# A normalising row carried to all partitions through memory: one matrix product, a store and a load in place of eight spreading products, in a conv and RG-LRU mixer layer

## The chip, the cores and the metric

The kernel runs on one core of a Trainium2 chip. Its time is the device time of the core in microseconds, the median of several executions. The engines are named as in the profile: PE is TensorE (its weight loads stand apart as PEld), DVE is VectorE, ACT is ScalarE, POOL is GpSimd and SP is SyncE. Each engine takes its instructions in order from a queue of its own, and so does each DMA queue (SyncE's, ScalarE's and GpSimd's).

## The reference

One layer, a sequence of 1024 tokens, 1024 channels, everything in float32. `c` is one vector, so `shift`, `scale` and `gate` are one number per channel, the same for all tokens.

```python
mod = silu(c) @ mod_w + mod_b
shift, scale, gate = split(mod, 3)
h = x * rsqrt(mean(x*x, axis=-1) + EPS) * norm_g * (1 + scale) + shift
cv, cg, cs, lx, ls = split(h @ w_in, 5)             # 1024 columns each
v = silu(layernorm(causal_depthwise_conv(cv * sigmoid(cg), 31 taps)))
y_conv = (v @ pw2_w + pw2_b) * silu(cs)
xs = causal_depthwise_conv(lx, 4 taps)              # RG-LRU: gates r, i from block-diagonal
y_lru = linear_scan(a(r), b(i, xs)) * silu(ls)      # products of xs, then a scan over tokens
x = x + (1 + gate) * (concat(y_conv, y_lru) @ w_out)
return rmsnorm(x, final_g)
```

What matters for this case is the first normalisation. It has one factor per token, 1/std = rsqrt(mean(x*x) + EPS), which depends on the whole row of x, and two numbers per channel, `gs` = norm_g * (1 + scale) and `shift`.

## The kernel before, in words

**Layout.** Channels lie on the 128 partitions and tokens along the free axis. x is eight tiles `x0` to `x7` of 128x1024, loaded transposed. A column tile of `h @ w_in` (128 output channels, called a slot: `cg0` is the first tile of the conv GLU gate, `cv0` of the conv value, and so on) is a sum over the eight channel tiles, in two halves of 512 tokens; each half fills one PSUM bank of 128x512. TensorE does an fp32 product as three products of a shorter type: an operand is cut into a high part and the rest (`whi`, `wlo` for weights, `uh`, `ul` for the input), and high by high, high by low and low by high are summed. A half of a slot is thus 8 x 3 = 24 products of 128x512. ScalarE makes `whi` (L336), VectorE or GpSimd the difference `wlo` (L363).

**Normalising after the product.** The first seven slots do not wait for 1/std. The tiles `uh_k` and `ul_k` hold gs * x, not normalised, made as soon as an x tile and its `gs` are there. The product of a slot with them is then multiplied, when it leaves its bank, by `rbc`: a tile of 128x1024 in which every partition holds the row of 1/std of all 1024 tokens. The part of `shift` is the same number for all tokens of an output channel; it comes from a sum of its own (`fsum` on VectorE and ScalarE, a product with ones into the bank `psbias`, copied to `bias`) and is added as a bias where the slot is used.

- The first four slots (`FIRST`: cg0, cv0, cg1, cv1, numbered 0 to 3) are computed while x and the weights are still being loaded (L774, `fw_mm`), each x tile going into all of them as it arrives. Slots 0 to 2 have two banks each, `first0_0`, `first0_1` and so on; slot 3 has one, `first3`, for its first half. With the bank of the token statistics, `token_stats`, all eight banks are taken. The second half of slot 3 is the bank `late` (24 products of L774), which follows when another bank is free. In the code this is "`(a, e) in cuts[i]`": true for the halves with a bank of their own; `len(cuts[i]) == 1` is slot 3.
- Their banks are emptied by VectorE (L363): `first_u<-first,rbc`, one multiply for each 128x512, and one for `late`.
- Three further slots (`NEXT`, `next4` to `next6`, banks `ps4_0` and so on, L494) go the same way, `next<-ps,rbc`.
- From the seventh slot on the input is the normalised one: VectorE writes x := x * gs * rbc (L355, `x<-x,gs,rbc`), ScalarE `uh` := x + shift (L344) and VectorE `ul` := x + shift - uh (L355), into the same sixteen tiles.

**1/std.** The squares of x are summed over the tiles; products with a column of ones (L910) give, for each of eight blocks of 128 tokens, one column of `token_stats`: token p of block b at partition p, column b. ScalarE takes the root, VectorE the reciprocal `st` (128x8). Then `spread_mm` (L916) brings it to all partitions:

```python
pe.matmul(psb()[:, o:o + P], st[:, b:b + 1].to_broadcast([P, P]), ident, start=True, stop=True)
```

The stationary operand is one column of `st` repeated 128 times, the moving operand the identity, so the result has the block's 128 values along the free axis, the same on every partition. Four of these fill the bank; ScalarE copies 128x512 to `rbc` (`rbc<-token_stats`), and the other four follow in the same bank.

**Order of the work.** The kernel is a list of operations, each with its engine, an estimated duration, what it reads and writes, and a priority (a number; `RSP` = -110, `HHP` = -40, `EVP` = -80 and the due times of the loads are such numbers). A list scheduler runs over them when the program is built: each time an engine is free in its model, it takes the ready operation with the lowest number. What comes out is a fixed order for every queue, and the assignment of the eight banks and of the 47 buffers of 128x1024 to the tiles in turn. On the chip only the order and the waits are left. So an operation whose number or duration is changed may change places with others, on other engines too. `lag` adds a delay to the estimate of an operation's result, `slack` lets an operation be put into a queue ahead of the time at which the model has its inputs ready.

**Weights and SyncE.** Weight tiles (`raw`, 512 KB), the tiles `modw` for `shift` and `gate` (512 KB, one dot product on VectorE each, L355 `modw<-modw,sc`), and small gate tiles (`graw`) come in on SyncE's queue in the order in which the scheduler puts them there.

Of the kernel before, what the change touches and what calls it, by code (L numbers as in the profile page):

```python
# [9 lines left out]
F32 = mybir.dt.float32  # L10
F32R = mybir.dt.float32r
AF = mybir.ActivationFunctionType
ALU = mybir.AluOpType

P = 128
D = 1024
T = 1024
KT = D // P
# [18 lines left out]
START = ((0, H), (H, T))  # L37
# [44 lines left out]
TAPP = 15  # L82
TP = -60
SCALE = ("DVE", "DVE", "DVE", "DVE", "DVE", "DVE", "DVE", "DVE")
SQP, RSP, BIP, HHP, HCH, EVP = -84, -110, -50, -40, 0.1, -80


LOADS = "s0 a0 w0 s1 b0 w1 x1 W2 s2 x2 s3 x3 W4 s4 x4 s5 x5 W6 s6 x6 s7 x7 h0 h1 h2 h3 h4 h5 h6 h7".split()
# [205 lines left out]
def hymba_layer(ctx: ExitStack, tc: tile.TileContext, xT, vecs, mod_w, w_first, w_in,  # L294
# [3 lines left out]
    act, dve, pool, pe, sp = nc.scalar, nc.vector, nc.gpsimd, nc.tensor, nc.sync  # L298
# [7 lines left out]
    dram = ctx.enter_context(tc.tile_pool(name="dram", bufs=1, space=bass.MemoryType.DRAM))  # L306
# [11 lines left out]
    S = Plan(pools)  # L318
# [11 lines left out]
    def ACT(prio, out, in_, func, n=T, bias=None, scale=None, accum=None, r=(), w=(),  # L330
            reserve=0, after=()):
        kw = {}

        def emit():
            if func == "copy":
                act.copy(out(), in_())  # L336
                return
            if bias is not None:
                kw["bias"] = bias
            if scale is not None:  # L340
                kw["scale"] = scale
            if accum is not None:
                kw["accum_out"] = accum
            act.activation(out=out(), in_=in_(), func=func, **kw)  # L344
        ptr = sum(x is not None and not isinstance(x, float) for x in (bias, scale))
        return S.op("ACT", a_cost(n, ptr) + (0.1 if accum is not None else 0), emit, prio, r, w,
                    table=SETS.get(func), reserve=reserve, after=after)
# [12 lines left out]
    def TT(prio, eng, out, a, b, op, n=T, r=(), w=(), reserve=0, after=()):  # L360
        e = dve if eng == "DVE" else pool
        return S.op(eng, d_cost(n) if eng == "DVE" else p_cost(n),
                    lambda: e.tensor_tensor(out=out(), in0=a(), in1=b(), op=op), prio, r, w,  # L363
                    reserve=reserve, lock=not in_psum(r), after=after)
# [16 lines left out]
    def DMA(prio, out, in_, nbytes, r=(), w=(), after=(), reserve=0):  # L381
        return S.op("SP", max(0.1, nbytes / 360e3),
                    lambda: sp.dma_start(out(), in_()), prio, r, w, after=after,
                    reserve=reserve)
# [17 lines left out]
    def part(b, a, e):  # L402
        if isinstance(b, Two):
            z = a // H
            return part(b.b[z], a - z * H, e - z * H)
        return lambda: b()[:, a:e]

    def halves(b, a, e):
        if isinstance(b, Two):
            return [(b.b[z], 0) for z in (0, 1) if z * H < e and a < z * H + H]  # L410
        return [(b, i) for i in range(b.parts) if i * (T // b.parts) < e
                and a < (i + 1) * (T // b.parts)]

    FULL_BYTES = P * T * 4
# [9 lines left out]
    ident = const.tile([P, P], F32, tag="ident", name="ident")  # L424
# [305 lines left out]
    psb = bank("token_stats")  # L730
    cuts = [START, START, START, START[:1]]
# [55 lines left out]
    for i, ld in enumerate(LOADS):  # L787
        p = due[ld] = i - 100.0
# [5 lines left out]
        elif ld[0] in "wW":  # L794
            nk = 1 + (ld[0] == "W")
            rw, hi, lo = fw[k - k % 2]
            n, o, js = nk * FW, (k % 2) * FW, range(k % 2, k % 2 + nk)
            keys = lambda b: [(b, j) for j in js]
            DMA(p, part(rw, o, o + n), lambda k=k, n=nk: w_first[:, k:k + n, :], n * P * 4,
                w=keys(rw))  # L800
            for j in range(k, k + nk):
# [4 lines left out]
                if j:  # L806
                    SUB(p, "DVE", fw_part(lo, j), fw_part(rw, j), fw_part(hi, j), FW,
                        r=[(rw, jj), (hi, jj)], w=[(lo, jj)])
# [35 lines left out]
    for k in range(KT):  # L844
        p = due[f"s{k}"]
# [8 lines left out]
        p = max(p, due[f"x{k}"] if k else p, due[f"w{k}"])  # L854
# [4 lines left out]
        for a, e in START if k < UK else ((0, T),):  # L859
            n = e - a  # L860
            hk = halves(x_, a, e)
            if k == 0 == a:
                o = TS(p, part(uh, a, e), part(x_, a, e), g, None, ALU.mult, n=n,
                       r=hk + [("gs", k)], w=halves(uh, a, e))
            else:
                o = ACT(p, part(uh, a, e), part(x_, a, e), AF.Copy, n, scale=g,
                        r=hk + [("gs", k)], w=halves(uh, a, e))
            if k == 0 == a:
                rw, hi, lo = fw[0]
                SUB(p, "DVE", fw_part(lo, 0), fw_part(rw, 0), fw_part(hi, 0), FW,  # L870
                    r=[(rw, 0), (hi, 0), *halves(uh, a, e)], w=[(lo, 0)])
# [3 lines left out]
                r=hk + halves(uh, a, e) + [("gs", k)], w=halves(ul, a, e)))  # L875
# [3 lines left out]
        for z in range(3 if k == 0 else 0):  # L879
            for i, ps in enumerate(psf):  # L880
                o = fw_mm(p, ps, i, uh, ul, k, START[:1], z=z)
# [3 lines left out]
        for ch, (a, e) in enumerate(START):  # L885
            for i, ps in enumerate(psf):
# [3 lines left out]
                for z in range(3) if k < ZK else (None,):  # L890
                    o = fw_mm(q + 0.003 * (z or 0), ps, i, uh, ul, k, ((a, e),),
                              after=[begun[i, a // H]] if k == 0 and a % H else [], z=z)
# [3 lines left out]
    for k in range(KT):  # L896
        p = SQP + k
# [7 lines left out]
    rbc = big_buf("rbc", parts=4)  # L905
    st, wk = ctile("st", KT), [psb]
# [3 lines left out]
            pe.matmul(psb()[:, b:b + 1], sq()[:, b * P:b * P + P], ones[:, 0:1],  # L910
                      start=k == 0 and b == 0, stop=k == len(sqs) - 1, skip_group_check=True)

    def spread_mm(a, e):
        for b in range(a // P, e // P):
            o = b * P - a
            pe.matmul(psb()[:, o:o + P], st[:, b:b + 1].to_broadcast([P, P]), ident, start=True,  # L916
                      stop=True)
    for k, sq in enumerate(sqs):
        S.op("PE", 0.23 * KT, lambda sq=sq, k=k: stats(sq, k), RSP, [sq], wk, columns=4 * P * KT,
             after=[last_u[LASTK - 1, 3, 0]] if k else [])  # L920
    root = ACT(RSP, lambda: st, lambda: psb()[:, :KT], AF.Sqrt, KT, bias=eps_t,
               scale=1.0 / D, r=wk, w=[("st", 0)])
    S.op("DVE", 0.2, lambda: dve.reciprocal(st, st), RSP, [("st", 0)], [("st", 0)])
    for a, e in START:
        spread = S.op("PE", 0.22 * ((e - a) // P), lambda a=a, e=e: spread_mm(a, e), RSP,
                      [("st", 0)], wk, columns=4 * (e - a))
        spread_out = ACT(RSP, part(rbc, a, e), part(psb, 0, e - a), "copy", e - a, r=wk,
                         w=halves(rbc, a, e))


    fsum, bias = big_buf("fsum", parts=2), ctile("bias", len(FIRST + NEXT))
# [3 lines left out]
    for k in range(KT):  # L935
        p = due[f"h{k}"]
# [6 lines left out]
        if k == 0:  # L943
            ACT(p, facc, fw_part(rw, k), AF.Copy, FW, scale=shift[:, k:k + 1],
                r=[(rw, 0), ("shift", k)], w=[(fsum, 0)])
# [3 lines left out]
        for i, s in enumerate(NEXT):  # L949
            to, rw = part(fsum, FW + i * P, FW + i * P + P), raw[s]  # L950
            src = lambda rw=rw, k=k: k3(rw)()[:, k, :]
            if k == 0:
                ACT(p + 5, to, src, AF.Copy, P, scale=shift[:, k:k + 1],
                    r=[(rw, k), ("shift", k)], w=[(fsum, 1)])
# [5 lines left out]
    def shift_mm():  # L960
# [5 lines left out]
        w=[("bias", 0)])  # L966
# [311 lines left out]
    for i, (s, ps) in enumerate(zip(FIRST, psf)):  # L1278
        j, p, bi = s[1] % KT, EVP + i, bias[:, i:i + 1]
        t = big_buf(f"first_u{i}", parts=4)  # L1280
        for a, e in START:
            tk, pk, n = halves(t, a, e), halves(ps, a, e), e - a
            if (a, e) in cuts[i]:
                TT(p - 4 * (len(cuts[i]) == 1), "DVE", part(t, a, e), part(ps, a, e),
                   part(rbc, a, e), ALU.mult, n, r=pk + halves(rbc, a, e), w=tk)
            else:
                late = bank("late")
                for k in range(KT):
                    fw_mm(RSP + 60 + 0.1 * k, late, i, uhs[k], uls[k], k, ((a, e),),
                          after=[spread], off=a)  # L1290
                TT(p, "DVE", part(t, a, e), part(late, 0, n), part(rbc, a, e), ALU.mult, n,
                   r=[late] + halves(rbc, a, e), w=tk)
            if s[1] < CG:
                if a == 0:
                    v[j] = big_buf(f"v{j}")
                STT(p + 3, apart(v[j], a, e), by_two(t, a, e), bi, by_two(sig[j], a, e), ALU.add,
                    ALU.mult, n, r=tk + halves(sig[j], a, e) + [("bias", 0)], w=[v[j]])
        if s[1] >= CG:
            ACT(p + 3, t, t, AF.Sigmoid, bias=bi, r=[t, ("bias", 0)], w=[t])
            sig[j] = t  # L1300
# [6 lines left out]
    for s in slots[4:]:  # L1307
# [10 lines left out]
        ps = Two(f"ps{n}")  # L1318
# [243 lines left out]
```

## Time and profile before

| what | value |
|---|---|
| median of 3 runs | 733.07 us (733.06 to 733.56) |
| the profiled execution | 733.2 us, of which 731.4 us is the span in the trace |
| mean granted TensorE clock | 0.997 |
| ACT busy, instructions | 461.3 us (63%), 620 |
| TensorE: products of L494 on the chain that ends last | 65% of the span |
| HBM traffic | 64.16 MB read, 12.58 MB written |

How to read the views: the page begins with the busy time of each engine, its share of the span and its number of instructions. The list of waits has, for an engine, the operation that waited, what it waited for, the total time, how often, and the longest. The chain is the work that ended last, followed back from the last instruction: the start in us, the length, the engine, what it wrote and the line. A timeline row has the start, the busy time of the row, the engine, line, operation and tiles, the shape and the number of instructions, and in brackets the idle time before it and what ended that. A matmul's duration in a timeline includes its passage through the pipeline (0.39 us), so successive ones overlap, and the distance from start to start is what one costs. A DMA row has the queue, the count, the size of one and the median time in us from issue to landing. A row of windows has the window, its length, the busy time and instruction count of PE, PEld, DVE, ACT and POOL, the granted TensorE clock, the busy share of the DMA engines and their rate in GB/s.

### The profile page before, as it was taken

Reading aid. Unit: us, or ns where it says so; the run is one execution under the profiler, and the core shown is the slowest. Engines: PE = TensorE matmul, PEld = TensorE weight load, DVE = VectorE, ACT = ScalarE, POOL = GpSimd, SP = SyncE. Lnnn points to the kernel's source line nnn. Section 1 sums busy time; section 2 is a strip of 40 time slices with the busy share of each in tenths; the row PEclk is TensorE's granted clock in tenths of the full one; section 3 lists DMA queues with packets and bytes.
Section 4 is the critical chain, followed back from the end, with each engine's and each line's share of the span. In section 5 each row is a group of like instructions: output and inputs, shape, how many; then the busy total and the mean of one; then the engine's idle time right before and its main releaser. Section 6 shows DMA issues by size and latency. Waiting matters only on the chain.

```text
span 731.4 us, 8952 instructions
## 1 busy us (share of the span) xinstructions
PE 722.9 (99%) x3284; PEld 601.5 (82%) x3284; DVE 640.4 (88%) x912; ACT 461.3 (63%) x620; POOL 98.0 (13%) x107
## 2 busy tenths in 40 slices
PE   9999999999999999999999999999999999999996
PEld 8888888888888888888888888888888888887885
DVE  6999999899999997688899995998999657899657
ACT  6660585776877977957867896835764334657421
POOL 0034012031222232233121100000000000000001
PEclk9999999999999999999999999999999999999998
DMA  9962023388699699699884536244233430622306
GB/s 330 407 209 87 0 82 87 99 201 186 145 250 244 133 214 222 149 219 197 195 180 92 106 88 193 89 170 160 105 110 117 171 116 0 231 87 87 116 1 230
DMA packets 37340, 111.59 MB, mean 153 GB/s; under 512 B 4144, under 2 KB 12848, under 8 KB 37296
## 3 DMA queue, kind: packets, MB, share of 16 engines
q1 hardware_dynamic: 23904, 75.97, 29.2%
q0 software_dynamic: 12528, 34.26, 26.2%
q10 hardware_dynamic: 864, 0.79, 0.3%
q8 instruction: 25, 0.41, 0.2%
q14 instruction: 19, 0.16, 0.1%
HBM read 64.16 MB, written 12.58 MB: 105 GB/s over the span
## 4 chain that ended last, share of the span: by engine, by line
PE 96%; DVE 2%; DMA 1%; SPq 0%; ACT 0%; issue 0%; DVEq 0%
PE ps L494 65%; PE first L774 5%; PE pbpw L605 3%; PE papw L605 3%; PE gate L1197 3%; PE pupw L605 3%; PE puout L605 2%; PE paout L605 2%; PE out L675 2%; PE pcpw L605 1%; PE pb0out L605 1%; PE pcout L605 1%; DVE o L355 1%; DMA fraw<-in_w_first_dram 1%; PE late L774 1%; PE out6b L675 1%
## 5 line engine op out<-in xcount | busy, mean ns | idle before, releaser
L494 PE MATMUL ps<-uh,whi 128*128 128x512 f32 x576 | 224.2, 389 | 0.0
L494 PE MATMUL ps<-ul,whi 128*128 128x512 f32 x576 | 224.1, 389 | 0.0
L494 PE MATMUL ps<-uh,wlo 128*128 128x512 f32 x576 | 224.1, 389 | 0.0
L494 PEld LDWEIGHTS ps<-ul,whi 128*128 128x128 f32 x576 | 108.1, 188 | 22.5
L494 PEld LDWEIGHTS ps<-uh,whi 128*128 128x128 f32 x576 | 108.1, 188 | 22.4
L494 PEld LDWEIGHTS ps<-uh,wlo 128*128 128x128 f32 x576 | 108.1, 188 | 22.4
L336 ACT CAST whi<-raw 128x1024 fp32r<-128x1024 f32 x46 | 48.0, 1049 | 44.2 <-PE ps L494 34.6
L344 ACT ACT_TABLE_LOAD x48 | 61.6, 1283 | 6.2 <-DVE sp8h L377 3.1
L368 POOL DMA_DIRECT2D es<-cq x45 | 40.4, 910 | 165.7 <-ACT cq L344 121.2
L363 DVE TENSOR_TENSOR wlo<-raw,whi 128x1024 fp32r<-128x1024 f32 x39 | 47.6, 1219 | 14.8 <-ACT whi L336 14.5
L355 DVE SCALAR_TENSOR_TENSOR cacc<-v,V,cacc 128x511 f32<-128x511 f32 (+14 forms) x75 | 55.6, 741 | 0.5
L355 DVE SCALAR_TENSOR_TENSOR caccs<-v,V,caccs 128x511 f32<-128x511 f32 (+6 forms) x70 | 52.2, 745 | 1.3
L355 DVE SCALAR_TENSOR_TENSOR caccs<-c,wsum,caccs 128x511 f32<-128x511 f32 (+6 forms) x70 | 51.9, 741 | 0.5
L368 POOL DMA_DIRECT2D oo<-co x42 | 38.3, 912 | 88.2 <-ACT co L344 46.5
L494 PE MATMUL ps<-yh,whi 128*128 128x512 f32 x128 | 49.8, 389 | 0.0
L494 PE MATMUL ps<-yl,whi 128*128 128x512 f32 x128 | 49.8, 389 | 0.0
L494 PE MATMUL ps<-yh,wlo 128*128 128x512 f32 x128 | 49.8, 389 | 0.0
L363 POOL TENSOR_TENSOR o<-fin,bc 128x256 f32<-128x256 f32 x4 | 2.8, 730 | 282.6 <-DMA out_dram<-o 277.5
L355 DVE SCALAR_TENSOR_TENSOR xs<-ps,V,xs 128x512 f32<-128x512 f32 (+3 forms) x48 | 35.8, 745 | 0.2
L344 ACT ACTIVATE cq<-v,V 128x511 f32<-128x511 f32 (+14 forms) x45 | 31.9, 709 | 0.0
L355 DVE SCALAR_TENSOR_TENSOR modw<-modw,sc 128x1024 f32<-128x1024 f32 x23 | 30.1, 1312 | 0.0
L344 ACT ACTIVATE cq<-c,wsum 128x512 f32<-128x512 f32 x42 | 29.9, 714 | 0.0
(378 smaller groups left out, 1450.3 us busy)
## 6 DMA issues: line engine op xcount, KB each, us to landing
raw<-in_w_in_dram SPq DMA_DIRECT2D x36, 512.0 KB, 4.4
modw<-in_mod_w_dram SPq DMA_DIRECT2D x24, 512.0 KB, 8.3
raw<-in_w_out_dram SPq DMA_DIRECT2D x10, 512.0 KB, 3.7
scsd<-scs SPq DMA_DIRECT2D x8, 512.0 KB, 4.7
acc<-in_xT_dram SPq DMA_DIRECT2D x8, 512.0 KB, 4.3
accd<-acc SPq DMA_DIRECT2D x8, 512.0 KB, 2.7
rawpw<-in_pw_dram SPq DMA_DIRECT2D x8, 512.0 KB, 3.4
scsr<-scsd SPq DMA_DIRECT2D x8, 512.0 KB, 5.1
```

Of the source, the lines that this page charges most:

```text
L336: act.copy(out(), in_())
L344: act.activation(out=out(), in_=in_(), func=func, **kw)
L355: dve.scalar_tensor_tensor(out=out(), in0=in0(), scalar=scalar, in1=in1(), op0=op0, op1=op1, accum_out=accum)
L363: lambda: e.tensor_tensor(out=out(), in0=a(), in1=b(), op=op), prio, r, w,
L368: return S.op("POOL", ISSUE, lambda: pool.dma_start(out(), a(), accum_op=ALU.add), prio, r, w, lag=RATE * n / T, after=after)
L494: pe.matmul(part(ps, a - off, b - off)(), k3(lhs)()[:, k, :], rhs[k]()[:, a:b], start=(k == 0 and lhs is wh and rhs is xh and (a - off) % ...
L605: pe.matmul(part(ps, 0, c1 - c0)(), half(*lhs)()[:, j * P:j * P + P], half(*rhs)()[:, c0:c1], start=start and j == 0 and z == 0, stop=j == ...
L675: pe.matmul(part(ps, a - off, e - off)(), k3(lhs)()[:, k, :], rhs()[:, i * H + a % H:i * H + a % H + e - a], start=k == KORD[0] and lhs is ...
L774: pe.matmul(part(ps, a - off, b - off)(), fw_part(lhs, k, i * P, i * P + P)(), rhs()[:, a:b], start=k == 0 and lhs is wh and rhs is xh, st ...
L1197: pe.matmul(ps(), lhs()[:, j, :], rhs()[:, c0:c1], start=st == 0, stop=st == 2)
```

## The change

What was eight spreading products in two groups, and two copies, becomes a path through memory:

- one product `turn` (L922), with `st` (128x8) as the stationary and the identity as the moving operand, gives `st` turned: 8 rows of 128, in columns 128 to 255 of the `token_stats` bank;
- ScalarE copies the 8x128 into the first 8 partitions of `rbc`, and its DMA queue stores them to a DRAM tile `rrowd` of 8x128, 4 KB;
- SyncE's queue loads `rrowd`, read as one row of 1024, into all 128 partitions of `rbc` (a partition broadcast, 512 KB written).

Slot 3's bank `first3` is now emptied by ScalarE, with a plain copy into `first_u3` that needs no `rbc`; VectorE multiplies that tile by `rbc` in place. The multiplies of the four slots get `slack = RBC_LAG`, 2.0. `HHP` goes from -40 to -56, so that the sums `uh` and `ul` of the seventh slot on have a lower number. The operations `after=[spread]` and `late=[... spread_out]` keep their names and now hang on the turn and its copy.

```diff
-SQP, RSP, BIP, HHP, HCH, EVP = -84, -110, -50, -40, 0.1, -80
+SQP, RSP, BIP, HHP, HCH, EVP = -84, -110, -50, -56, 0.1, -80
+RBC_LAG = 2.0
...
-    def spread_mm(a, e):
-        for b in range(a // P, e // P):
-            o = b * P - a
-            pe.matmul(psb()[:, o:o + P], st[:, b:b + 1].to_broadcast([P, P]), ident, start=True,
-                      stop=True)
...
-    for a, e in START:
-        spread = S.op("PE", 0.22 * ((e - a) // P), lambda a=a, e=e: spread_mm(a, e), RSP,
-                      [("st", 0)], wk, columns=4 * (e - a))
-        spread_out = ACT(RSP, part(rbc, a, e), part(psb, 0, e - a), "copy", e - a, r=wk,
-                         w=halves(rbc, a, e))
+    def turn():
+        pe.matmul(psb()[:KT, P:2 * P], st, ident, start=True, stop=True)
+    spread = S.op("PE", 0.2, turn, RSP, [("st", 0)], wk, columns=4 * P)
+    row, flat = lambda: rbc()[:KT, :P], dram.tile([KT, P], F32, tag="rrow", name="rrowd")
+    spread_out = ACT(RSP, row, lambda: psb()[:KT, P:2 * P], "copy", P, r=wk, w=[(rbc, 0)])
+    S.op("ACT", 0.3, lambda: act.dma_start(flat, row()), RSP, [(rbc, 0)], [("rrowd", 0)], lag=0.1)
+    DMA(RSP, rbc, lambda: flat.rearrange("b p -> (b p)").partition_broadcast(P), FULL_BYTES,
+        r=[("rrowd", 0)], w=[rbc])
...
             if (a, e) in cuts[i]:
-                TT(p - 4 * (len(cuts[i]) == 1), "DVE", part(t, a, e), part(ps, a, e),
-                   part(rbc, a, e), ALU.mult, n, r=pk + halves(rbc, a, e), w=tk)
+                alone = len(cuts[i]) == 1
+                if alone:
+                    ACT(RSP, part(t, a, e), part(ps, a, e), "copy", n, r=pk, w=tk)
+                TT(p - 4 * alone, "DVE", part(t, a, e), part(t if alone else ps, a, e),
+                   part(rbc, a, e), ALU.mult, n, r=(tk if alone else pk) + halves(rbc, a, e),
+                   w=tk).slack = RBC_LAG
```

The line numbers of the changed kernel are one higher than those of the kernel before, from the new constant to about L910. The order of the instructions, in three places:

TensorE, from the first spread to the start of `late` (`firstI_1` is the bank of slot I's second half, `fhi`, `flo` its weights, the numbers at the end count buffers). Before:

```order
L916 MATMUL token_stats_120<-ident_79,st_100 128x128 x4
L774 MATMUL first1_1_206<-uh6_399,fhi6_350 128x512
...
L774 MATMUL first1_1_206<-ul7_456,fhi6_350 128x512
L916 MATMUL token_stats_120<-ident_79,st_100 128x128 x4
L774 MATMUL first2_1_209<-uh6_399,fhi6_350 128x512
...
L774 MATMUL first2_1_209<-ul7_456,fhi6_350 128x512
L774 MATMUL late_557<-uh0_169,fhi0_154 128x512
```

After:

```order
L922 MATMUL token_stats_121<-ident_79,st_100 8x128
L775 MATMUL first1_1_207<-uh6_400,fhi6_351 128x512
...
L775 MATMUL first1_1_207<-ul7_457,fhi6_351 128x512
L775 MATMUL first2_1_210<-uh6_400,fhi6_351 128x512
...
L775 MATMUL first2_1_210<-ul7_457,fhi6_351 128x512
L775 MATMUL late_547<-uh0_170,fhi0_155 128x512
```

Two groups of four products are gone and one product stands where the first group stood; the two pieces of six products follow each other, then `late`.

VectorE, where it begins to multiply by `rbc` (`modw` is a dot product of a modulation tile). Before:

```order
L355 SCALAR_TENSOR_TENSOR modw3_418,macc_93<-modw3_418,sc_151 128x1024
L363 TENSOR_TENSOR first_u3_555<-first3_188,rbc_532 128x512
L939 TENSOR_TENSOR shift_91<-macc_93,V_77 128x1
L355 SCALAR_TENSOR_TENSOR modw4_428,macc_93<-modw4_428,sc_151 128x1024
L363 TENSOR_TENSOR first_u0_575<-first0_0_177,rbc_532 128x512
...
L363 TENSOR_TENSOR first_u2_601<-first2_1_209,rbc_532 128x512
L363 TENSOR_TENSOR first_u3_555<-late_557,rbc_532 128x512
L355 SCALAR_TENSOR_TENSOR fsum_477<-fraw2_165,shift_91,fsum_477 128x512
L939 TENSOR_TENSOR shift_91<-macc_93,V_77 128x1
L363 TENSOR_TENSOR next4_645<-ps4_0_607,rbc_532 128x512
```

After:

```order
L356 SCALAR_TENSOR_TENSOR modw3_419,macc_93<-modw3_419,sc_152 128x1024
L356 SCALAR_TENSOR_TENSOR modw4_429,macc_93<-modw4_429,sc_152 128x1024
L364 TENSOR_TENSOR first_u0_585<-first0_0_178,rbc_528 128x512
...
L364 TENSOR_TENSOR first_u2_607<-first2_1_210,rbc_528 128x512
L364 TENSOR_TENSOR first_u3_474<-late_547,rbc_528 128x512
L364 TENSOR_TENSOR first_u3_474<-first_u3_474,rbc_528 128x512
L364 TENSOR_TENSOR next4_638<-ps4_0_599,rbc_528 128x512
L939 TENSOR_TENSOR shift_91<-macc_93,V_77 128x1 x2
```

The multiply of slot 3's first half has moved from the head of the multiplies to behind that of `late`, and reads its own tile in place of the bank; the dot product `modw4` now stands ahead of the first instruction that needs `rbc`, and `shift` and `fsum` behind the multiplies.

VectorE, some 40 instructions on, where the normalised input of the seventh slot is made (`next6` is the last slot on the un-normalised input). Before:

```order
L363 TENSOR_TENSOR next6_800<-ps6_0_753,rbc_532 128x512
L355 SCALAR_TENSOR_TENSOR fsum_477<-raw6_486,shift_91,fsum_477 128x128
L355 SCALAR_TENSOR_TENSOR x5_294<-x5_294,gs_90,rbc_532 128x512
L355 SCALAR_TENSOR_TENSOR x6_333<-x6_333,gs_90,rbc_532 128x512 x2
L355 SCALAR_TENSOR_TENSOR x7_373<-x7_373,gs_90,rbc_532 128x512 x2
L355 SCALAR_TENSOR_TENSOR ul0_185<-x0_124,shift_91,uh0_169 128x512 x2
L355 SCALAR_TENSOR_TENSOR ul1_228<-x1_158,shift_91,uh1_219 128x512 x2
L355 SCALAR_TENSOR_TENSOR v0_852<-first_u1_586,bias_101,first_u0_575 128x2x256
```

After:

```order
L364 TENSOR_TENSOR next6_792<-ps6_0_746,rbc_528 128x512
L356 SCALAR_TENSOR_TENSOR fsum_486<-raw5_465,shift_91,fsum_486 128x128
L356 SCALAR_TENSOR_TENSOR ul0_186<-x0_125,shift_91,uh0_170 128x512
L356 SCALAR_TENSOR_TENSOR fsum_486<-raw6_502,shift_91,fsum_486 128x128
L356 SCALAR_TENSOR_TENSOR x4_267<-x4_267,gs_90,rbc_528 128x512
L356 SCALAR_TENSOR_TENSOR ul0_186<-x0_125,shift_91,uh0_170 128x512
L356 SCALAR_TENSOR_TENSOR x5_295<-x5_295,gs_90,rbc_528 128x512
L356 SCALAR_TENSOR_TENSOR ul1_229<-x1_159,shift_91,uh1_220 128x512
```

The sums `ul` of the first tiles now begin before all tiles of x have been multiplied, and the two kinds take turns.

## The prediction

> **What bounds the kernel now.** I read the busy shares and the list of TensorE's waits first, to see whether anything but TensorE sets the time.
>
> ```profile
> span 731.4 us, 8952 instructions
> PE 722.9 (99%) x3284; PEld 601.5 (82%) x3284; DVE 640.4 (88%) x912; ACT 461.3 (63%) x620; POOL 98.0 (13%) x107
> PE token_stats L740 <- DVE ones L427: 1.1, 1, 1.1
> PE puout L605 <- ACT eout L336: 0.7, 1, 0.7
> PE finbc L698 <- DVE finss L363: 0.2, 1, 0.2
> ```
>
> TensorE is busy for 99% of the span and, between its start and 660 us, waits for nobody. So a microsecond taken out of TensorE's queue comes off the end, as long as nobody behind it becomes late; and a microsecond that another engine loses costs nothing until TensorE has to wait for it. Next comes the chain of waits in the stretch that the change touches (start, length, what).
>
> ```profile
> 43.63 1.68 PE token_stats L910 x16
> 45.30 1.51 PE first L774 x6
> 46.82 0.92 PE token_stats L916 x8
> 47.73 1.39 PE first L774 x6
> 49.12 0.89 PE token_stats L916 x8
> 50.01 1.39 PE first L774 x6
> 51.40 5.71 PE late L774 x24
> 57.11 28.56 PE ps L494 x126
> ```
>
> The whole stretch is TensorE's. The two pieces of L916 are the products that spread 1/std: each `x8` is four products, two records each. From 57.11 us 126 products take 28.56 us, 0.227 us each. Last, the timeline of TensorE at the first spread and at the start of `late` (start, duration).
>
> ```profile
> 46.65 1.08 PE L916 MATMUL token_stats<-ident,st 128*128 128x128 f32 x8
> 47.49 0.47 PE L774 MATMUL first<-uh,fhi 128*128 128x512 f32 x1
> ...
> 51.01 0.40 PE L774 MATMUL first<-ul,fhi 128*128 128x512 f32 x1
> 51.38 0.50 PE L774 MATMUL late<-uh,fhi 128*128 128x512 f32 x1
> 51.72 0.40 PE L774 MATMUL late<-uh,flo 128*128 128x512 f32 x1
> ```
>
> From start to start four spread products take 0.84 us, 0.21 each. `late` starts 0.37 us after its predecessor and its second product 0.34 us later, where 0.227 is the rule: 0.14 + 0.11 = 0.25 us, too short for the list of waits, in which TensorE waited for VectorE to empty the third slot's bank, as the next rows show (VectorE, then GpSimd).
>
> ```profile
> 50.63 0.69 DVE L363 TENSOR_TENSOR first_u<-first,rbc 128x512 f32<-128x512 f32 x1
> 52.84 4.01 DVE L363 TENSOR_TENSOR first_u<-first,rbc 128x512 f32<-128x512 f32 x6 [0.31 <-PE late L774]
> 57.15 0.69 DVE L363 TENSOR_TENSOR first_u<-late,rbc 128x512 f32<-128x512 f32 x1 [0.30 <-PE late L774]
> 57.76 2.31 DVE L355 SCALAR_TENSOR_TENSOR fsum<-fraw,shift,fsum 128x512 f32<-128x512 f32 x1
> 60.00 2.35 DVE L939 TENSOR_TENSOR shift<-macc,V 128x1 f32<-128x1 f32 x1
> 62.59 0.69 DVE L363 TENSOR_TENSOR next<-ps,rbc 128x512 f32<-128x512 f32 x1 [0.25 <-PE ps L494]
> 51.67 10.66 POOL L363 TENSOR_TENSOR wlo<-raw,whi 128x1024 fp32r<-128x1024 f32 x4 [2.23 <-ACT whi L336]
> ```
>
> **The change, TensorE.** Removed: both spread groups, 0.92 + 0.89 = 1.81 us of chain. Added: one product of the same moving width with 8 columns of weights. The trace has no such product; the nearest is one of the four, 0.21 us, and the change of kind after it costs 0.08 (a group's 0.92 less its 0.84): 0.29. The bounds are 0.21 and half a group, 0.46. Gone is also `late`'s 0.25: the bank is emptied by ScalarE before the spread, and VectorE's multiply of it comes after `late`. This stall may leave nothing (0) or all of it (0.25); I take all, since the bank's last product is some nine products ahead of the statistics at 43.63 us. Sum: -1.81 + 0.29 - 0.25 = **-1.77 us**; with the bounds from -1.35 to -1.85. All other products are the same, in another order.
>
> **When the row arrives.** ScalarE with one dot product of VectorE, the DMA rows for sizes near these (median us from issue to landing), and the busiest stretch of the DMA engines:
>
> ```profile
> 42.02 0.72 ACT L344 ACTIVATE fsum<-fraw,shift 128x512 f32<-128x512 f32 x1 [2.64 <-DVE shift L939]
> 46.75 0.39 ACT L336 CAST ghi<-graw 128x256 fp32r<-128x256 f32 x1
> 47.77 0.59 ACT L336 COPY rbc<-token_stats 128x512 f32<-128x512 f32 x1 [0.52 <-PE token_stats L916]
> 66.53 1.22 DVE L355 SCALAR_TENSOR_TENSOR modw<-modw,sc 128x1024 f32<-128x1024 f32 x1
> 87.33 0.15 ACT L336 COPY bias<-psbias 128x7 f32<-128x7 f32 x1
> out_dram<-o ACTq DMA_DIRECT2D x6, 128.0 KB, 1.9
> rawpw<-in_pw_dram SPq DMA_DIRECT2D x8, 512.0 KB, 3.4
> scsr<-scsd SPq DMA_DIRECT2D x8, 512.0 KB, 5.1
> x<-in_xT_dram SPq DMA_DIRECT2D x7, 512.0 KB, 10.1
> 20.00:30.00 10.00, 10.00 (x45) 8.14 (x45) 10.00 (x19) 7.04 (x12) 0.00 (x0) 1.00 1.03 406
> ```
>
> The turn starts where the first spread did, 46.65, and is out at about 46.95. ScalarE's copy of 8 rows lies between the 7-column copy (0.15) and the old one (0.59); say 0.3, to 47.3. In its queue the `ghi` cast comes next (0.39), so the store is issued at 47.7 and lands 1.9 later, at 49.6. SyncE issues the load then; it lands 3.4 (quiet queue) to 5.1 us later (the store and load of `scs`, the kernel's own tile read back). I take 3.5, so D = 53.1; the bounds are 53.0 and 54.7. Three weight loads and one gate load are ahead of it on that queue, as before.
>
> VectorE has the next dot product (`modw`, 1.22 us, formerly behind the third slot's multiply) ahead of its wait for the row: it starts where that multiply did, 50.63, and ends at about 51.8. Then VectorE stands still for 1.3 us until D, with every later VectorE instruction queued behind. TensorE waits for those only through the banks. `late` takes the bank that ScalarE empties, the first bank of the next slot is that of the statistics (free at 47.3), and the second starts 1.77 us before 57.11 + 24 x 0.227 = 62.55, so at 60.8; its bank is free one multiply (0.66) after D, at 53.8. Cover: 7 us.
>
> The narrower cover is VectorE's own backlog. After D it does eight multiplies: 4.01 + 0.69 + 0.69, 5.3 us, to 58.4. In the run before it took up the next slot's first multiply at 62.59, after 0.25 of idle time, having lost 1.6 us in `fsum` and 2.2 in `shift`, which ran 2.31 and 2.35 us while GpSimd's four subtractions ran. So D may be as late as 62.4 - 5.3 = **57.1** before VectorE falls behind its former place; 4.0 us after my D.
>
> One multiply changes kind there: the third slot's first half is now read from SBUF. By its PSUM row it takes 0.69; as an SBUF operation amid GpSimd's four it can take 2.35 like `shift`, and I charge it up to 1.7 us more, which moves 57.1 to 55.4, still past both bounds of D. The Trainium skill (SBUF — State Buffer, "SBUF: two separate sides") says that a VectorE operation with two SBUF inputs and a GpSimd operation that reads SBUF lock each other out for a whole instruction. By that rule the multiply is blocked whenever it meets a subtraction, and the sum stays; the rows agree, 2.35 for one column.
>
> **Edits at no cost.** ScalarE: a copy of 128x512 more (0.59) goes into the 2.64 us idle before 42.02; one copy of 128x512 less, a shorter one for the other and a store issue more follow, ahead of the 24.72 us that it idles before 79.59 (first of the rows below). If that cover were gone, 0.59. SyncE: its wait for the store holds back until 49.6 what is queued behind: two `modw` loads (one was ahead of it before) and the later weight loads. The sixth `modw` then lands by 49.6 + 0.5 + 10.1 = 60.2 at worst and its dot product ran at 66.53. The sums:
>
> ```profile
> 79.59 0.73 ACT L344 ACTIVATE uh<-x,shift 128x512 fp32r<-128x512 f32 x1 [24.72 <-PE ps L494]
> 94.83 8.04 DVE L355 SCALAR_TENSOR_TENSOR ul<-x,shift,uh 128x512 fp32r<-128x512 f32 x12
> 96.16 0.39 PE L494 MATMUL ps<-ul,whi 128*128 128x512 f32 x1
> 103.64 0.39 PE L494 MATMUL ps<-ul,whi 128*128 128x512 f32 x1
> ```
>
> The sums moved ahead: all sixteen `ul` are still there. The first of the twelve here ends at 94.83 + 0.74 = 95.57 and is used at 96.16, the last ends at 102.87 and is used at 103.64: covers of 0.59 and 0.77 us. TensorE now comes 1.77 us earlier, but six products (1.36 us) more stand ahead of the last `ul` product, and VectorE is up to 0.8 us earlier: of the 1.6 + 2.2 = 3.8 us that it lost to GpSimd, 1.3 of waiting for the row and 1.7 of the third slot's multiply remain. Last cover: 0.77 - 1.77 + 1.36 + (0 to 0.8) = 0.4 to 1.2. I take no cost; the bounds are 0 and, if none of the move ahead helped, 1.77 - 0.59 = 1.2 us.
>
> **The rivals.** *1, the forecast:* -1.77 on the profiled 733.2 us (its span is 731.4, so 1.8 lies around it), giving 731.4; that run stands 0.13 above the median of 733.07, so **731.3**. *2, the sums of the seventh slot are late:* TensorE waits up to 1.2 us in 85 to 100 us, gain 0.6 to 1.4, time 731.7 to 732.5. For it: covers of 0.6 us, VectorE 88% busy. Against: the earlier sums. *3, slower, the row is late:* all 128 partitions read the same 4 KB. At the 406 GB/s of the row above 512 KB take 1.29 us of the 3.4; at an n-th of that rate D = 49.6 + 2.1 + 1.29n. It costs from D = 57.1 (n = 4.2) and the gain is used up at 58.9 (n = 5.6); with n = 8, D = 62.0, 3.1 us slower, 736.2; with n = 16, 746.5. A load like the queued `x` (10.1) gives D = 59.7 and 733.9. For it: no row shows such a load. Against: every load from memory here, written by the kernel or not, lands in 3.4 to 5.1 us on a queue that isn't full. The Trainium skill (DMA: Bandwidth & Descriptors, "Latency and other measured facts") reports that copies whose rows lie a large power of two apart fall from 207 to 103 GB/s, channels aliasing being its guess. A source that doesn't move at all could be such a case; at half the rate, n = 2, D would be 54.3 and nothing is lost. *4, the change saves less than it says:* the lone product costs like half a group and `late` still waits, gain 1.35, time 731.7.
>
> **How the numbers follow.** 1 has 0.67, 2 has 0.14, 3 has 0.10 (nothing in the trace speaks for a fourth of the rate), 4 has 0.09. The range holds 1, 4 and 2: from 730.7, which is the bound of -1.85 and 0.5 for scatter (the runs of before lie 0.5 apart), to 732.9, which is 4's gain of 1.35 less the whole 1.2 of 2. About 0.2% (1.5 us) is what a measurement of this kernel can tell from no change; 731.6 is that line. 1 lies past it by 0.3, 4 and part of 2 on either side of it within their scatter: faster 0.71, same 0.18, slower 0.11 (3, and a part of 2 with a late row).
>
> **What would show it.** In the changed profile: one L922 product of two records in place of sixteen; `late` 0.227 us after its predecessor, starting near 49.6; the load of `rbc` landing near 53 and the first multiply there, with VectorE idle about 1.3 us before it; the slot's second bank and the products of 85 to 100 us without a wait of TensorE. Wrong: a wait of TensorE for `first_u`, for `psbias` or for `ul` before 105 us, a landing after 57.1, or a wait that is new after 105 us, where the order of the convolutions has shifted too.

## The result and the profile after

The changed kernel takes 731.99 us (median of 22 runs, 731.19 to 732.66); the kernel before took 733.59 us in 22 runs beside them (732.99 to 734.46). The ratio is 0.9977, with a 95% interval of 0.9970 to 0.9984: 1.69 us less (1.60 between the two medians). The forecast was 1.77 us less.

The span and the longest of TensorE's waits in the changed kernel:

```profile
span 730.4 us, 8922 instructions
...
PE token_stats L741 <- DVE ones L428: 1.1, 1, 1.1
PE first L775 <- DVE ul L356: 0.8, 1, 0.8
```

Its chain (start, length, what):

```profile
44.31 1.68 PE token_stats L911 x16
45.99 1.51 PE first L775 x6
47.50 0.31 PE token_stats L922 x2
47.82 2.96 PE first L775 x12
50.77 5.44 PE late L775 x24
56.21 29.92 PE ps L495 x132
```

The two spread pieces are gone, one turn stands there, and `late` has fallen from 5.71 to 5.44 us. One wait is new, 0.8 us of `first` for `ul`; it lies at 13 us, while x and the weights are still being loaded, where the order of no queue has changed. The forecast named a wait for `ul` before 105 us as a sign of being wrong; it meant the sums of the seventh slot, and there is none there. The statistics thus start 0.68 us later, and this shift has to be taken out before the stretches are compared. From the start of the statistics to the end it is 731.4 - 43.63 = 687.77 us before and 730.4 - 44.31 = 686.09 after: 1.68 us less. The span by itself shows only 1.0. The runs, which include the start, agree with 1.68.

The path of the row, in the timelines of ScalarE, SyncE and VectorE of the changed kernel:

```profile
47.85 0.26 ACT L337 COPY rbc<-token_stats 8x128 f32<-8x128 f32 x1 [0.32 <-PE token_stats L922]
48.14 0.53 ACTq L926 DMA_DIRECT2D rrowd<-rbc  x1
49.90 0.33 SPq L384 DMA_DIRECT2D rbc<-rrowd  x1
51.08 1.22 DVE L356 SCALAR_TENSOR_TENSOR modw<-modw,sc 128x1024 f32<-128x1024 f32 x1
54.05 3.68 DVE L364 TENSOR_TENSOR first_u<-first,rbc 128x512 f32<-128x512 f32 x6 [1.75 <-DMA rbc<-rrowd]
57.65 0.68 DVE L364 TENSOR_TENSOR first_u<-late,rbc 128x512 f32<-128x512 f32 x1
58.25 1.60 DVE L364 TENSOR_TENSOR first_u<-first_u,rbc 128x512 f32<-128x512 f32 x1
61.69 0.69 DVE L364 TENSOR_TENSOR next<-ps,rbc 128x512 f32<-128x512 f32 x1 [1.84 <-PE ps L495]
```

VectorE stands still for 1.75 us until the row is there, does its eight multiplies and then waits 1.84 us for TensorE. TensorE waits for nothing here.

### The profile page after: what moved, and what is told of

Same layout as the page of the kernel before. It is cut to its first block, busy times and chain, and to the rows that moved or that the text cites. A ratio compares the mean times of both kernels' runs of the same rounds, so it can differ in the third digit from the quotient of the medians.

```text
span 730.4 us, 8922 instructions
## 1 busy us (share of the span) xinstructions
PE 721.1 (99%) x3270; PEld 599.7 (82%) x3270; DVE 637.5 (87%) x912; ACT 461.1 (63%) x620; POOL 97.9 (13%) x107
## 4 chain that ended last, share of the span: by engine, by line
PE 96%; DVE 2%; DMA 1%; ACT 0%; SPq 0%; issue 0%; DVEq 0%; ACTq 0%
PE ps L495 66%; PE first L775 5%; PE papw L606 3%; PE pbpw L606 3%; PE gate L1197 3%; PE pupw L606 3%; PE puout L606 2%; PE paout L606 2%; PE out L676 2%; PE pcpw L606 1%; PE pb0out L606 1%; PE pcout L606 1%; DVE o L356 1%; DMA x<-in_xT_dram 1%; PE late L775 1%; PE out6b L676 1%
## 5 line engine op out<-in xcount | busy, mean ns | idle before, releaser
L364 POOL TENSOR_TENSOR wlo<-raw,whi 128x1024 fp32r<-128x1024 f32 x7 | 18.2, 2627 | 88.8 <-ACT whi L337 88.8
```

## The experiments

Two numbers are given for each kernel: the median against the runs of before beside it, and, from the profile, the time from the first row of the statistics products in TensorE's timeline to the end of the span, which leaves out the scatter of the loads at the start. The second is of one execution, with the span given to 0.1 us. By that count the kernel before has 687.93 us (731.4 - 43.47) and the changed one 686.25 (730.4 - 44.15).

| kernel | statistics to `late` | `late` to `ps` | statistics to end | against before | ratio of the runs |
|---|---|---|---|---|---|
| before | 7.91 | 5.57 | 687.93 | | |
| changed | 6.46 | 5.44 | 686.25 | -1.68 | 0.9977 (0.9970 to 0.9984) |
| changed, again | 6.46 | 5.44 | 686.25 | -1.68 | 0.9975 (0.9964 to 0.9985) |
| copy alone | 7.74 | 5.44 | 687.59 | -0.34 | 0.9995 (0.9986 to 1.0004) |
| sums ahead alone | 7.89 | 5.57 | 687.83 | -0.10 | 0.9999 (0.9990 to 1.0008) |
| changed, no copy | 6.46 | 6.16 | 687.31 | -0.62 | 1.0012 (1.0000 to 1.0024) |
| changed, sums not ahead | 6.46 | 5.44 | 687.88 | -0.05 | 1.0000 (0.9992 to 1.0009) |
| row later by 4.0 us | 6.46 | 5.44 | 686.18 | -1.75 | 0.9980 (0.9970 to 0.9989) |
| row later by 8.0 us | 6.46 | 5.44 | 689.47 | +1.54 | 1.0011 (1.0002 to 1.0019) |
| row later by 9.3 us | 6.46 | 5.44 | 690.71 | +2.78 | 1.0033 (1.0021 to 1.0045) |
| 4-byte store, no turn | 5.92 | 5.45 | 690.60 | +2.67 | 1.0043 (1.0031 to 1.0055) |
| turn on VectorE | 5.92 | 5.44 | 685.73 | -2.20 | 0.9967 (0.9954 to 0.9980) |
| turn on VectorE, again | 5.93 | 5.44 | 685.79 | -2.14 | 0.9972 (0.9961 to 0.9983) |

**One part alone: ScalarE's copy of slot 3's bank.** The kernel before, with

```diff
-                TT(p - 4 * (len(cuts[i]) == 1), "DVE", part(t, a, e), part(ps, a, e),
-                   part(rbc, a, e), ALU.mult, n, r=pk + halves(rbc, a, e), w=tk)
+                alone = len(cuts[i]) == 1
+                if alone:
+                    ACT(RSP, part(t, a, e), part(ps, a, e), "copy", n, r=pk, w=tk)
+                TT(p - 4 * alone, "DVE", part(t, a, e), part(t if alone else ps, a, e), ...)
```

> The kernel before, with only slot 3's bank emptied by ScalarE and multiplied by rbc from SBUF; both spread groups stay. Theory A (the prediction's term): the 0.25 us by which late waited for VectorE goes, its start and second product come 0.227 us after the one ahead; time -0.25 us (0.2 to 0.3) against before, ratio 0.9997. Rival B: the multiply that now reads SBUF runs beside GpSimd's subtractions, VectorE loses up to 1.7 us and a sum of the seventh slot comes late: 0 to +1 us. Rival C: this copy carries most of the change's gain: -1 us or more.

Its TensorE, at the start of `late`:

```profile
51.95 0.39 PE L774 MATMUL late<-uh,fhi 128*128 128x512 f32 x1
52.18 0.39 PE L774 MATMUL late<-uh,flo 128*128 128x512 f32 x1
```

`late` starts 0.23 us after its predecessor (at 51.72), where it was 0.37, and its second product comes 0.23 us later, where it was 0.34. The stall is gone: at these two steps 0.14 + 0.11, the forecast's 0.25; over the whole stretch the table has 0.17 us ahead of `late` and 0.13 in it, 0.30 in all. The runs can't tell this from nothing, the profile can.

**One part alone: the sums moved ahead.** The kernel before with `HHP` at -56.

> The kernel before with HHP at -56 alone: the sums uh and ul stand earlier in the queues, the spread stays. Theory A: the sums had 0.59 to 0.77 us of cover in the kernel before and TensorE waited for none of them, so nothing is gained: 0 us against before (-0.3 to +0.3), and the move is worth something only where TensorE comes 1.7 us earlier. Rival B: it is worth something by itself, -0.5 us or more. And on the scatter of the start: TensorE's wait of 0.7 to 1.4 us for ul in the first 20 us, in the profile of every kernel but the one before, should be here too if it is the loads' scatter, and not here if it comes with the change.

By both counts it is as theory A has it. The wait of the start is here too, though no queue's order is changed there:

```profile
PE first L774 <- DVE ul L355: 0.8, 1, 0.8
```

**One part undone: the copy.** The changed kernel with VectorE emptying slot 3's bank from PSUM, as before.

> The changed kernel without ScalarE's copy: VectorE multiplies slot 3's bank by rbc, as before the change. The order now gives late the bank of the statistics, and slot 3's bank to the first half of the next slot (ps4_0). Theory A: TensorE comes to ps4_0 at about 56.2 us, the row lands at about 54.0 and the bank is empty one multiply later, 54.7; 1.5 us of cover, nothing lost: -1.6 us against before, as the whole change. Rival B: the copy is what lets the row be late; without it TensorE waits for the row at late or at ps4_0: the gain falls by 1 to 4 us, time -0.6 to +2.4 us.

VectorE, SyncE and TensorE of that kernel:

```profile
52.00 0.33 SPq L384 DMA_DIRECT2D rbc<-rrowd  x1
56.26 4.28 DVE L364 TENSOR_TENSOR first_u<-first,rbc 128x512 f32<-128x512 f32 x7 [1.37 <-PE late L775]
57.01 0.50 PE L495 MATMUL ps<-uh,whi 128*128 128x512 f32 x1 [0.55 <-DVE first_u L364]
```

Rival B holds. The banks were as theory A read them, but its 1.5 us of cover was for a row at 54. Here the load was issued 3.6 us after the store, not 1.8, and the row came 2.2 us later. (VectorE's row names `late` as what ended its wait; the load, issued at 52.00 with 4.1 us to its landing, ends at 56.1, and the multiply follows it as closely as in the changed kernel.) The runs scatter: they lie between 732.3 and 736.6 us, where those of the changed kernel lie within 1.5. By the medians against before the copy is worth 2.1 us in this kernel (0.47 more without it, 1.60 less with it), and 0.3 in the other: it lets the row be late.

**One part undone: the sums.** The changed kernel with `HHP` at -40.

> The changed kernel with HHP at -40, as before the change: the sums uh and ul of the seventh slot stand later in the queues. Theory A: their cover was 0.59 to 0.77 us and TensorE comes 1.6 to 1.8 us earlier, so TensorE waits about 1 to 1.6 us for ul between 85 and 100 us, and most of the gain is lost: -0.1 to -0.7 us against before. Rival B: VectorE's own gain (it lost 3.8 us to GpSimd before, 0.9 after) makes the sums earlier by themselves: -1.5 to -1.7 us, and no wait of TensorE there.

```profile
67.00 0.69 DVE L364 TENSOR_TENSOR next<-ps,rbc 128x512 f32<-128x512 f32 x1 [0.34 <-PE ps L495]
94.69 0.50 PE L495 MATMUL ps<-ul,whi 128*128 128x512 f32 x1 [1.44 <-DVE ul L356]
```

Theory A, at its upper end and a little past it: TensorE waits 1.44 us for `ul`, and all of the gain is gone. In this execution the row landed 2.0 us later than in the changed kernel's (56.03), but this has no part in the wait: at 67.00 VectorE has caught up and waits for TensorE (first row).

**The row made late.** One, two and three further loads of the same form stand in SyncE's queue ahead of that of `rbc`; every other queue keeps its order (`n` stands for their number).

```diff
...
+    def row_load():
+        for i in range(n):
+            sp.dma_start(ahead[i], flat.rearrange("b p -> (b p)").partition_broadcast(P))
+        return sp.dma_start(rbc(), flat.rearrange("b p -> (b p)").partition_broadcast(P))
...
```

> The changed kernel with one more load of the same form (512 KB, every row from the 4 KB of rrowd, into a scratch tile in memory) in SyncE's queue between the store and the load of rbc; every other queue keeps its order. It should move the landing D from 54.05 to 55.4 to 56.7 us. Theory A (the prediction's): VectorE has 1.84 us of idle time behind its eight multiplies and about 1 us more before 85 us, and the ul sums have 0.55 us of cover, so a later row costs max(0, D - 57.4): nothing, -1.6 us against before. Rival B: VectorE is as good as the bound and each us past 55.9 costs one: 0 to 0.8 us lost. Rival C: only the bank of ps4_1 counts, nothing is lost before D = 60.9.

> The same with two loads ahead: D at 56.7 to 59.3. Theory A: max(0, D - 57.4), 0 to 1.9 us lost, time -1.6 to +0.3 us against before. Rival B: 0.8 to 3.4 us lost. Rival C: nothing lost, -1.6 us.

> The same with three loads ahead: D at 58.0 to 61.9. Theory A: max(0, D - 57.4), 0.6 to 4.5 us lost, time -1 to +2.9 us against before, TensorE waiting for ul at 88 to 104 us or for the bank of ps4_1. Rival B: 2.1 to 6 us lost. Rival C: up to 1 us lost. Theory D, on top of A: where TensorE stands still for 2 us or more the granted clock falls behind it (as in the kernel without the turn, 0.67 and 0.50 in the 4 us after a wait of 2.25 us), and 1.5 to 2 us more are lost.

The loads went slower than I took them to. Counted from the start of the statistics, the row came 4.0, 8.0 and 9.3 us later than in the changed kernel, which is D = 58.1, 62.0 and 63.3 on that kernel's clock. VectorE and TensorE of the first, then of the second, then of the third, and the third in stretches of 1 us (TensorE's busy time and count first, the granted clock third from the end):

```profile
57.96 3.68 DVE L364 TENSOR_TENSOR first_u<-first,rbc 128x512 f32<-128x512 f32 x6 [5.71 <-DMA rbc<-rrowd]
62.15 0.68 DVE L364 TENSOR_TENSOR first_u<-first_u,rbc 128x512 f32<-128x512 f32 x1
```

```profile
62.70 1.89 DVE L364 TENSOR_TENSOR first_u<-first,rbc 128x512 f32<-128x512 f32 x3 [9.66 <-DMA rbc<-rrowd]
63.45 0.50 PE L495 MATMUL ps<-uh,whi 128*128 128x512 f32 x1 [1.12 <-DVE first_u L364]
95.22 0.50 PE L495 MATMUL ps<-ul,whi 128*128 128x512 f32 x1 [0.46 <-DVE ul L356]
```

```profile
64.00 0.79 PE L495 MATMUL ps<-uh,whi 128*128 128x512 f32 x1 [2.41 <-DVE first_u L364]
```

```profile
63.00:64.00 1.00, 0.00 (x1) 0.00 (x1) 0.75 (x2) 0.00 (x0) 0.00 (x0) 0.86 0.96 389
64.00:65.00 1.00, 1.00 (x2) 0.83 (x3) 1.00 (x2) 0.00 (x0) 0.00 (x0) 0.50 1.03 422
...
66.00:67.00 1.00, 1.00 (x4) 0.81 (x3) 1.00 (x3) 0.00 (x0) 0.00 (x0) 0.50 0.67 274
67.00:68.00 1.00, 1.00 (x5) 0.78 (x5) 1.00 (x2) 0.00 (x0) 0.00 (x0) 0.94 0.14 57
```

At D = 58.1 nothing is lost; rival B is out. At 62.0 3.2 us are lost, in the bank's wait of 1.12 and later waits for `fsum` and `ul`, of which one is shown; rival C is out too. At 63.3 it is 4.5 us. The chains of the second and the third say why: from the row's landing to the `ul` that TensorE then takes up they hold VectorE's queue alone, 37.10 us in both.

```profile
62.70 4.88 DVE first_u L364 x8
...
99.80 26.62 PE ps L495 x116
```

```profile
63.25 4.88 DVE first_u L364 x8
...
100.35 26.62 PE ps L495 x116
```

So past some point a later row costs one for one. The loss begins at 62.0 - 3.2 = 63.3 - 4.5 = 58.8, an estimate, against 57.4 in theory A. Theory D's fall of the clock is there, 0.50 from 64 to 67 us, but it does not come on top: VectorE sets the time, and the slowed TensorE has none of the later waits in its list. The profiled execution of the second kernel is one of the slowest three of its 12 (736.07 us); its median, 734.46, is only 0.6 us above before.

**The turn without TensorE, by the store.** `st` goes to memory as it is, 1024 pieces of 4 bytes.

```diff
...
+    spread_out = spread = S.op("ACT", 0.3, lambda: act.dma_start(flat.rearrange("b p -> p b"), st), RSP,
+                 [("st", 0)], [("rrowd", 0)], lag=0.1)
...
```

> The changed kernel without the turn product and without the 8x128 copy: the ACT queue stores st (128x8) to the row directly, turned by the addresses, 1024 pieces of 4 bytes; the load stays. Theory A: the product with its two changes of kind cost 0.5 us of TensorE (0.54 by the trace of after against 0.29 forecast), the store has its cover: -2.1 us against before (-1.9 to -2.3). Theory A0 (the forecast's 0.29 is right and the rest is chance): -1.9. Rival B: 1024 small pieces take 4 us or more longer than the store of 8 rows, the row lands after 59 us, TensorE waits at ps4_1 or for ul: -1 us to slower than before. The store starts at about 47.2 us in place of 48.1.

```profile
47.07 0.38 ACTq L922 DMA_DIRECT2D rrowd<-st  x1
57.16 0.33 SPq L384 DMA_DIRECT2D rbc<-rrowd  x1
63.22 0.50 PE L495 MATMUL ps<-uh,whi 128*128 128x512 f32 x1 [2.25 <-DVE first_u L364]
```

TensorE did gain its half microsecond (5.92 in the table), but the store took 10 us in place of 1.8, and rival B holds.

**The turn without TensorE, by VectorE.** Blocks of 32x32 are transposed, and the store's addresses put them in order; of the 128 pieces of 128 bytes that it writes, the first 32 in memory are the row that the load reads.

```diff
...
+    S.op("DVE", 0.1, lambda: dve.transpose(stt, stw), RSP, [("st", 0)], [("stt", 0)])
+    flat = dram.tile([32, P], F32, tag="rrow", name="rrowd")
+    spread_out = spread = S.op(
+        "ACT", 0.3, lambda: act.dma_start(flat.rearrange("r (q c) -> q r c", c=32), stt), RSP,
...
```

> The changed kernel with st turned by VectorE (one transpose of 32x32 blocks, 128x32) in place of TensorE's product and ScalarE's copy; the store writes 128 pieces of 128 bytes, of which the first 4 KB are the row. Theory A: TensorE loses the product and its two changes of kind, 0.54 us by the trace of after; VectorE gains one instruction of 0.2 us; the store starts at about 48 us as before and takes the 2 us of the 4 KB store: time -2.2 us against before (-1.9 to -2.5), 0.5 better than the change. Theory A0 (the forecast's 0.29): -1.9 to -2.0. Rival B: the store of 128 pieces lands later as that of 1024 pieces did (10 us): from 57.4 on it costs us for us, and the time is that of the change or worse.

> The changed kernel beside the one that turns st on VectorE, on one chip: -1.5 to -1.8 us against before, as its 22 runs gave.

> The kernel that turns st on VectorE, once more beside the changed kernel: 0.5 us less than that (0.3 to 0.7), -2.0 to -2.4 us against before. If the first run's 0.7 us beside the change was chance: no difference from the change beyond 0.2.

VectorE, SyncE and TensorE in the profile of its first run:

```profile
47.76 0.20 DVE L923 STREAM_TRANSPOSE stt<-stw 128x32 f32<-128x32 f32 x1
50.35 0.33 SPq L384 DMA_DIRECT2D rbc<-rrowd  x1
47.12 0.39 PE L775 MATMUL first<-ul,fhi 128*128 128x512 f32 x1
47.35 0.40 PE L775 MATMUL first<-uh,fhi 128*128 128x512 f32 x1
54.91 3.68 DVE L364 TENSOR_TENSOR first_u<-first,rbc 128x512 f32<-128x512 f32 x6 [3.54 <-DMA rbc<-rrowd]
```

Theory A holds in the profiles: no product stands between the two `first`, and TensorE is at `late` 0.54 and 0.53 us earlier after the start of the statistics than in the changed kernel. The store of 128 pieces lets the load go 2.4 us after its issue, half a microsecond later than that of 8. The runs are less clear. The first time the median was 731.51 us, 2.3 below before. The second time, side by side with the changed kernel, it was 731.69 beside 731.76 (the latter 1.80 below before, at the edge of what was expected): the expected 0.5 us did not show, and the case of no difference beyond 0.2 came out. Over all runs, from several chips, the medians are 731.65 (12) and 731.93 us (29), the means 0.33 us apart with a standard error of 0.13. So this kernel is some 1.9 to 2.3 us below before; that it gains the half microsecond over the changed one is shown by the profiles, not by the runs.

## Why the prediction was right

**The spread groups, 1.81 us:** right. From the statistics to `late` it is 1.45 us less. With 0.17 of that for the stall (copy alone) and 0.53 given back for the turn, 1.81 are left; the kernels without the turn say the same directly (7.91 - 5.92 = 1.99, of which 0.17 is the stall).

**The turn, 0.29 us: the term that was mis-sized.** TensorE's timeline in the changed kernel:

```profile
47.10 0.40 PE L775 MATMUL first<-ul,fhi 128*128 128x512 f32 x1
47.43 0.38 PE L922 MATMUL token_stats<-ident,st 128*8 128x128 f32 x2
47.75 0.51 PE L775 MATMUL first<-uh,fhi 128*128 128x512 f32 x1
48.09 0.40 PE L775 MATMUL first<-uh,flo 128*128 128x512 f32 x1
```

From 47.10 to 48.09 are 0.99 us, where two steps of 0.227 would do: 0.53 too much, as the kernels without it also give, and above the bound of 0.46. Only 0.32 lies between its start and the next; 0.10 is lost ahead of it and 0.11 behind the first product after it. I had charged the change of kind once, at 0.08, taken from the end of a group of four. The 0.10 ahead looks like a wait for `st`, which the row of the weight load names:

```profile
47.43 0.10 PEld L922 LDWEIGHTS token_stats<-ident,st 128*8 128x8 f32 x2 [0.36 <-DVE st L919]
```

But `st` was done at 47.15 (46.95 + 0.20). In the seven profiles with the turn the load starts 0.2 to 0.3 us after `st`, now more and now less, but always 0.32 to 0.33 after the start of the product ahead, while in the kernel before it started 0.04 us after `st`. So it is not that wait; why the load of 8 columns starts so late stays open.

**The stall of `late`, 0.25 us:** right at its two steps; 0.30 over the whole stretch in the kernel with the copy alone.

**The row's landing.** The forecast had it 6.45 us after the start of the turn (46.65 to 53.1); it was 6.62 (47.43 to 54.05), with 0.7 us to the issue of the store where 1.05 was taken, 1.8 for the store where 1.9 was and 4.1 for the load where 3.5 was. VectorE stood still for 1.75 us, not 1.3. That the wide load is an ordinary one was right, and the rival of the late row fell; but the experiments show its mechanism. The point from which the row costs was put at 57.1, which is 57.8 on the changed kernel's clock: the run at 58.1 lost nothing, and 58.8 is the estimate, so the point was put too early by 1.0. The break-even of 58.9 would be 59.6 there; the row at 62.0 was past it, with a loss of 3.2 against a gain of 1.7. What the forecast did not weigh is the scatter: over the seven profiles of the changed kernel and its variants with the same store, the first load of the row was issued 1.8 to 3.6 us after the store.

**The sums.** The last `ul` now ends at 103.38 (VectorE below, 97.33 + 6.05) and the `ul` product that follows starts at 104.10: the cover is 0.72 us, within the forecast's 0.4 to 1.2.

```profile
97.33 6.05 DVE L356 SCALAR_TENSOR_TENSOR ul<-x,shift,uh 128x512 fp32r<-128x512 f32 x9
104.10 0.39 PE L495 MATMUL ps<-ul,whi 128*128 128x512 f32 x1
```

The price if the move had not helped was put at up to 1.2 us; undone, it is 1.4 us by the wait, 1.6 by the table and 1.75 by the medians, all past that bound.

**The multiply from SBUF** took 1.60 us, in the charged 0.69 to 2.35; with the turn on VectorE it took 2.83, past that bound.

**The time itself.** 731.3 was forecast and 731.99 measured. Of these 0.69 us, 0.52 lie in the base: the three runs shown of before had a median of 733.07, the 22 have 733.59. So the three lay low among the runs of before. The profiled one of them has no wait at the start, while the changed kernel shows one in its profile and so do, at 0.8 us, the two kernels in which only one part of the change was made; that this wait is the 0.52 is not shown. The rest is the turn's 0.24, less what the stall gave more. The terms as measured give -1.81 + 0.53 - 0.30 = -1.58 us; the 0.10 by which the profiles differ beyond that lies behind `late`, where the kernels without a wait differ by as much among themselves.

**Whose gain it is.** All of it is TensorE's, from the spread. The copy and the sums moved ahead, which alone bring 0.3 and nothing that shows, are what keeps it: without the one or the other the kernel is no faster than before.

## What to carry to other kernels

Where one engine is busy for 99% of the span, a product taken out of its queue comes off the end one for one, but every cover behind it shrinks by the same amount: look for the covers that are thinner than the gain, and move those operations ahead in the same change. A path through memory is cheap if its worst landing, not its mean, is covered; a copy that empties a bank without waiting for the row buys this cover. Before a span is compared with another, subtract the time at which the loads have let the bound engine start: here it hid 0.7 of 1.7 us.

## What the runs showed of the hardware

- **A small product among others costs more than its own time.** One fp32 product of 8 columns among products of 0.227 us cost 0.53 us, 0.21 of it outside its own 0.32.
- **The clock fell after waits of 2.25 and 2.41 us.** In the two kernels with these waits the granted clock was 0.50 for about 3.4 us, from 1.5 us behind the end of the first wait and from 0.3 us ahead of the end of the second, and a product took 0.43 us from start to start; after 0.55, 1.12 and 1.44 us it stayed at 1.00. A wait of 2.41 us thus put TensorE back by about 4, an estimate (2.41 and half of 3.4). The Trainium skill (TensorE: Matmul & The Clock Gate, "Part 1: The HAM clock gate") puts the fall behind an idle window of about 3.4 us and the rise behind a busy window of the same length; the length of the slow stretch agrees with the second, but here a shorter wait was enough for the fall, and the measurement decides.
- **The size of the pieces of a store.** 4 KB in 1024 pieces of 4 bytes let the load go after 10.1 us; in 8 rows after 1.8 to 3.6; 16 KB in 128 pieces of 128 bytes after 2.4 and 2.2.
- **A row of 4 KB read by all 128 partitions** lands like any 512 KB: 4.0 us in the changed kernel, where the medians of other loads of that size lie between 3.4 and 10.1; alone it shows no sign of a slow source. With two and three further such loads queued ahead the DMA engines were fully and 95% busy from 57 to 61 us and moved 231 and 198 GB/s, where fully busy from 20 to 30 us they moved 406 in the kernel before; whether the shared row or the writing of the further copies to memory slows them is not shown.
- **VectorE beside GpSimd.** The same multiply, both inputs in SBUF, took 1.44 to 2.83 us while GpSimd's subtractions ran, and 0.68 at 62.15 us in the kernel whose row came late, behind the last of them (GpSimd's row there):

```profile
51.34 10.23 POOL L364 TENSOR_TENSOR wlo<-raw,whi 128x1024 fp32r<-128x1024 f32 x4 [1.33 <-ACT whi L337]
```
